# Low-part key products and cumulative-sum broadcasts over 128 rows instead of 64, in a two-layer hybrid decoder kernel

## The chip, the core and the metric

The kernel runs on one core of a Trainium2 chip. The core has a matrix engine (TensorE, PE in the rows, its weight loads PEld), VectorE (DVE), ScalarE (ACT), GpSimd (POOL), and a queue engine for transfers (SyncE, SP). The metric is the device time of one execution in microseconds, as the median of several runs.

## The reference, cut to what matters

Two layers run for a prompt of 512 tokens and a sample group of 8 x 4 = 32 tokens. The three branches of a layer share one normalised input `h`:

```python
A  = indexer-selected sparse GQA softmax attention (top-256 keys per query, 16 query heads, 4 key heads of 64)
B  = multi-scale causal pooling
C  = Mamba-2 SSD (32 heads of 64, state 128, chunks of 128, exact scan)
x += gate1 * (sum_b sigmoid(G_b) * (branch_b @ w_branch_b)) @ w_out
x += gate2 * ((silu(g) * a) @ ffn_down),   [a, g] = causal_dwconv3(h2 @ ffn_up)
```

Three places matter here. In the attention a score is `q . k` over 64 elements. In the indexer, which chooses the keys, a score is the sum over 8 heads of `w * relu(qi . ki)`, again over 64 elements. In the SSD branch the decay between two tokens of a chunk is `exp(cs[t] - cs[s])`, where `cs` is the cumulative sum of `dt * a` of one head over the tokens of its chunk.

## The kernel before

Tensors lie with channels on the 128 partitions and the 544 tokens along the row. Every large product is made in float32r with both operands split in a high and a low part: `gemm` (line 336 holds its matmul) makes `wh*xh`, `wh*xl` and `wl*xh` for each of 8 blocks of the contraction, in two halves of 272 columns. For each weight tile SP loads `raw`, ACT rounds it to `wh` (line 177) and DVE subtracts to get `wl` (line 322).

A layer runs `project`, `ssd`, `pool_branch`, `attention`, `merge_out`, `ffn`. Beside the products of a stage run side chains, written as generators in lanes; `pump` advances each lane by some steps before every product. While the SSD's input and gate weights are multiplied, the lanes make the indexer scores (`scores`) and the SSD heads (`ssd_chain`, `ssd_sample`). The top-k search of the indexer (lines 805 and 806, DVE) runs later, beside the branch products. A scheduler in the framework then sets the final order on each engine from its own model of durations; tiles come from rings of buffers, with a wait where a buffer is still in use.

The products that the change touches have a contraction of only 64:

- **Attention, line 1368** (`attn_scores`). A unit is one block of 128 queries (`i` = 0 to 3), one pair of key heads `p` and one pair of query rows `rp`: 16 units a layer. For each of its four query heads, `qs` holds the high part of the query in 64 partitions and the low part in the other 64. Line 1367 multiplies all 128 rows with `khh`, in which the high part of the keys stands twice. Line 1368 adds the high part of the query times the low part of the keys, `klo`, over the 64 partitions `es` of this head, into the same PSUM bank. `klo` holds two heads in one tile, one in each half. The number of columns is `nk` = 128 * (i + 1).
- **Indexer, line 783** (`scores`). The same construction: line 782 over 128 rows with `ikh`, line 783 over 64 rows with `ikl`, at 256, 384 and 512 columns, for 8 heads.
- **SSD, lines 977 and 1048**. `csT` holds the cumulative sums, one head to a row, high parts in rows 0 to 31 and low parts in rows 32 to 63. One column of `selc`, a matrix of zeros and ones, taken as a weight for all 128 output rows, broadcasts the row of one head to all partitions: 512 columns for the prompt (line 977, then subtracted from on DVE in line 981), 32 for the sample group (line 1048, eight in a row).

The softmax of a unit runs on DVE (mask and maximum, line 1373, which also frees the PSUM tile), ACT (line 1376) and DVE again; then PE transposes the result (line 1390) and multiplies with the values (line 1395). PSUM tiles `psg` come from a ring of two, shared by these scores and by `gemm`. Units 0 to 4 of a layer have one gate product each beside them (`filler`), and from unit 8 on the attention of the sample group runs beside them. The low keys are made by DVE in line 1260, four per layer.

Of the kernel before, what the change touches and what calls it, by code (L numbers as in the profile page):

```python
# [36 lines left out]
HC = T // 2  # L37
# [66 lines left out]
class Prog:  # L104
# [90 lines left out]
    def consts(self):  # L195
# [14 lines left out]
        nc.vector.memset(self.mean_w[:, 1:2], 1.0 / 512)  # L210
        self.selc = self.cp.tile([64, 32], F32R, name="selc")
        nc.vector.tensor_copy(self.selc, c[:64, C_SEL:C_SEL + 32])
        self.oh = self.cp.tile([32, 8, 64], BF16, name="oh")
# [21 lines left out]
    def ada(self, l, s, first=False):  # L235
        """modulation columns of two of the six chunks, in four groups of two channel tiles each."""
        nc, a = self.nc, self.a
# [102 lines left out]
    def gemm2(self, srcs, rhs, done=None):  # L340
        """two products, both for the first half of the tokens before the second half."""
        nc = self.nc
        self.pump()
        self.pump()
        K = len(rhs)
        ws, self.pre = self.pre or [self.weights(src, K * 128) for src in srcs], None
        os_ = [self.G() for _ in srcs]
        for c in range(2):
            for (wh, wl), o in zip(ws, os_):
                for k in range(K):  # L350
                    xh, xl = rhs[k]
                    for w, x, first, last in ((wh, xh, True, False), (wh, xl, False, False), (wl, xh, False, True)):
                        nc.tensor.matmul(o[:, c, :HC], w[:, k * 128:(k + 1) * 128], x[:, c * HC:(c + 1) * HC],  # L353
                                         start=(k == 0 and first), stop=(k == K - 1 and last))
            if done:
                done(os_, c)
        return os_
# [79 lines left out]
    def gemm_norm(self, l, srcs, rhs, gate, second):  # L437
        """the last two products of a sum into x, and the normalisation that follows."""
        st = {}

        def done(os_, c):
            for z, o in enumerate(os_):
                self.resid(l, 6 + z, o, gate, (c,))
            if second is not None:
                self.norm(l if second else l + 1, second, c, st)
        self.gemm2(srcs, rhs, done)
# [79 lines left out]

    # ---- attention projections, indexer scores
    def project(self):
# [17 lines left out]
        self.project_qi()  # L546
        # v, token-major
        wv = [self.weights(a["wv"][l, z], 1024) for z in range(2)]
# [70 lines left out]
    def dt_chain(self, kd):  # L619
# [73 lines left out]
        ct = self.csT = self.t("csT")  # L693
        cr = ct.bitcast(F32R)
        for so, do in ((o[:32, :], slice(0, 512)), (o2[:32, :32], slice(512, T))):
            self.copy("dt_chain20", cr[:32, do], so)
            self.E("dt_chain19").tensor_tensor(cr[32:64, do], so, ct[:32, do], op=OP.subtract)
        yield

    def scores(self):  # L700
# [3 lines left out]
        self.tp_ = []  # L704
        # sample group
        qs = self.t("qis")
# [55 lines left out]
        yield  # L762
        # prompt: both parts of a query head stacked against the high part of the keys
        khi, klo = self.t("ikh"), self.t("ikl")
# [6 lines left out]
        for hd in range(8):  # L771
# [6 lines left out]
            for i in PO:  # L778
# [3 lines left out]
                nc.tensor.matmul(ps[:, :nk], xr[:, ts], khr[:, :nk], start=True, stop=False)  # L782
                nc.tensor.matmul(ps[:, :nk], xr[o_, ts], klr[o_, :nk], start=False, stop=True)  # L783
                r = self.t("rel")
# [45 lines left out]

    # ---- SSD branch
    def conv(self, o, par, wb, nt, bb, st, so, i, width):
        """depthwise causal convolution of one channel tile; o: [128, 2, HC] in PSUM."""
        nc = self.nc
# [120 lines left out]
    def ssd_chain(self, q, jj, xs):  # L955
# [18 lines left out]
        for e in range(2):  # L974
            hd = 2 * j + e
            ps = self.P("ssd_chain2")
            nc.tensor.matmul(ps, self.selc[:, hd:hd + 1].to_broadcast([64, 128]), csr[:64, :512], start=True, stop=True)  # L977
            d = self.t("seg")
# [48 lines left out]
    def ssd_sample(self, q):  # L1027
# [19 lines left out]
        for i in range(8):  # L1047
            nc.tensor.matmul(ps[:, i * 32:(i + 1) * 32], self.selc[:, 8 * g + i:8 * g + i + 1].to_broadcast([64, 128]),
                             csr[:64, 512:], start=True, stop=True)
        ecs, mt = self.t("secs"), self.t("smt")  # L1050
# [88 lines left out]

    # ---- pooling branch  # L1140
    def pool_branch(self):
# [95 lines left out]

    # ---- attention
    def attention(self):
# [5 lines left out]
        for p in range(2):  # L1245
            nc.scalar.dma_start(kt[p], a["o_k"][l, p])
            nc.scalar.dma_start(vt[p][:, :512].rearrange("p (i c) -> p i c", i=2),
                                a["o_v"][l, p * 256:(p + 1) * 256].rearrange("(i p) c -> p i c", p=128))
        # high and low parts of the keys
        khh, klo = [], []  # L1250
        self.knew = self.s([128, 2, 32], "knew", bufs=1)
        for p in range(2):
            self.E("attention1").tensor_copy(self.knew[:, p, :], kt[p][:, 512:])
            lo = self.t("klo").bitcast(F32R)
            for e in range(2):
                hi = self.t("khh").bitcast(F32R)
                for z in range(2):
                    self.copy("attention9", hi[64 * z:64 * z + 64, :512], kt[p][64 * e:64 * e + 64, :512])
                s_ = slice(64 * e, 64 * e + 64)
                self.E("attention2").tensor_tensor(lo[s_, :512], kt[p][s_, :512], hi.bitcast(F32)[s_, :512], op=OP.subtract)  # L1260
                khh.append(hi)
            klo.append(lo)
        q = []
# [32 lines left out]
        self.E("attention6").tensor_scalar(nsq8, rq[:, 0:4], -0.125, None, op0=OP.mult)  # L1296
        # sample queries, normalised and laid out block-diagonally
        bc = [self.t("qbc0"), self.t("qbc1")]
# [44 lines left out]
    def attn_scores(self, u, q, khh, klo, sq8, nsq8):  # L1343
# [18 lines left out]
        for e in range(2):  # L1362
            ps = self.G()
            es = slice(64 * e, 64 * e + 64)
            for r2 in range(2):
                zs = slice((2 * e + r2) * 128, (2 * e + r2) * 128 + 128)
                nc.tensor.matmul(ps[:, r2, :nk], qr[:, zs], khh[2 * p + e][:, :nk], start=True, stop=False)  # L1367
                nc.tensor.matmul(ps[:, r2, :nk], qr[es, zs], klo[p][es, :nk], start=False, stop=True)  # L1368
            for r2 in range(2):
# [72 lines left out]
    def sample_scores(self, b, kv, P):  # L1442
        """rows of the scores: page half, key head pair, key head, token, query head."""
        nc = self.nc
# [79 lines left out]

    # ---- output projection of the merged branches
    def merge_out(self):
# [15 lines left out]

    # ---- feed-forward
    def ffn(self):
# [81 lines left out]
def _tiles(w):  # L1626
    """[K, M] -> [M/128, 128, K/128 * 128], tile rows in order of the contraction index within its block."""
    K, M = w.shape
# [7 lines left out]
def prep(x_prompt, x_sample, c_prompt, c_sample, cache_k, cache_v, cache_kidx, page_table,  # L1636
# [8 lines left out]
    out["cT"] = np.concatenate([c_prompt, c_sample], 0).T.reshape(8, 128, 9).transpose(1, 0, 2)  # L1645
    wa = w_ada.reshape(L, 4, 2, 128, 3, 2, 4, 256)  # l, k pair, k, row, set, chunk, group, column
    out["w_ada"] = wa.transpose(0, 4, 6, 1, 3, 2, 5, 7).reshape(L, 3, 16, 128, 1024)
# [119 lines left out]
```

## Time and profile before

| | |
|---|---|
| time, median of three runs | 3312.31 us (3304.55 to 3320.29) |
| span of the profiled execution | 3323.4 us |
| mean granted TensorE clock, share of full speed | 0.967 |
| PE / DVE / ACT / POOL busy | 97% / 67% / 38% / 27% |
| chain that ended last | PE 82%, DVE 4% |

The page gives the span of one execution. No separate time of that execution is listed; the span lies 11 us above the median and 3 us above the longest of the three runs. In the rows below, "64\*128" behind an instruction of PE means that its weights cover 64 rows and 128 columns of the array, "128\*128" all of it; this is called its form. PEclk is the granted clock: 1.00 is 2.4 GHz and 0.50 is 1.2 GHz.

### The profile page before, as it was taken

The page shows a single profiled execution, that of the slowest core. Times are in us where ns is not written, and L with a number is a line of the kernel's source. Part 1 is how long each engine was busy: PE and PEld are TensorE (multiplying, and loading weights), DVE is VectorE, ACT ScalarE, POOL GpSimd, SP SyncE. Part 2 cuts the span into 40 slices and gives each one's busy share as a digit, 9 for nine tenths or more (in the row PEclk, how much of TensorE's full clock was granted, in tenths as well). Part 3 has the DMA queues.
Part 4 walks back from the last instruction along what each step waited for, and adds up shares of the span by engine and source line. Part 5 has one row for each costly group of instructions (what it writes and reads, how often), then busy time and mean ns, then how long its engine had stood idle before and what let it go on. Part 6 is the DMA issues. An engine that isn't in the chain of part 4 may idle for free.

```text
span 3323.4 us, 62987 instructions
## 1 busy us (share of the span) xinstructions
PE 3240.0 (97%) x24322; PEld 2872.7 (86%) x24322; DVE 2229.5 (67%) x4817; ACT 1262.6 (38%) x2228; POOL 892.1 (27%) x1271
## 2 busy tenths in 40 slices
PE   7999999999999999999999999999999999999999
PEld 5987898999896598888989877888999956999999
DVE  4687778679876656444566777786799866564554
ACT  3344434333234534323343344433342345253432
POOL 1363435521021002111123544355120200031211
PEclk8998999999998899999999989999999989999999
DMA  6332323345532433545334323233343324333332
GB/s 218 108 100 75 103 76 102 115 130 186 167 109 91 157 124 113 149 141 151 115 107 118 89 80 101 84 99 113 97 126 115 92 90 161 116 74 87 86 96 76
DMA packets 303102, 376.85 MB, mean 113 GB/s; under 512 B 177362, under 2 KB 186930, under 8 KB 302802
## 3 DMA queue, kind: packets, MB, share of 16 engines
q1 hardware_dynamic: 116514, 315.94, 29.4%
q10 hardware_dynamic: 181216, 42.05, 6.2%
q0 software_dynamic: 5072, 14.83, 1.2%
q8 instruction: 192, 3.15, 0.4%
q14 instruction: 108, 0.88, 0.1%
HBM read 330.34 MB, written 33.79 MB: 110 GB/s over the span
## 4 chain that ended last, share of the span: by engine, by line
PE 82%; DVE 4%; issue 1%; ACT 1%; POOL 1%; DMA 1%; ACTq 0%; SPq 0%; POOLq 0%; DVEq 0%
PE psg L336 61%; PE psb L253 2%; PE psg L353 2%; PE psb L1395 1%; PE psg L1368 1%; PE psa L1390 1%; PE psg L1367 1%; PE psb L1005 1%; PE psa L1087 1%; PE psg L1455 1%; PE psb L991 1%; PE psb L1014 1%; DVE wl L322 1%; PE psa L977 1%; PE psa L783 1%
## 5 line engine op out<-in xcount | busy, mean ns | idle before, releaser
L177 ACT ACTIVATE wh<-raw 128x1024 fp32r<-128x1024 f32 (+2 forms) x434 | 424.8, 980 | 1208.7 <-PE psg L336 930.7
L336 PE MATMUL psg<-hh,wh 128*128 128x272 f32 x4064 | 868.5, 294 | 4.2 <-ACT cacc L838 3.3
L336 PE MATMUL psg<-hl,wh 128*128 128x272 f32 x4064 | 858.9, 291 | 0.0
L336 PE MATMUL psg<-hh,wl 128*128 128x272 f32 x4064 | 857.3, 291 | 0.0
L322 DVE TENSOR_TENSOR wl<-raw,wh 128x1024 fp32r<-128x1024 f32 (+2 forms) x434 | 510.8, 1177 | 356.4 <-ACT wh L177 346.8
L336 PEld LDWEIGHTS psg<-hh,wh 128*128 128x128 f32 x4064 | 643.9, 190 | 60.9 <-issue 31.8
L336 PEld LDWEIGHTS psg<-hl,wh 128*128 128x128 f32 x4064 | 645.7, 190 | 19.0 <-issue 17.4
L336 PEld LDWEIGHTS psg<-hh,wl 128*128 128x128 f32 x4064 | 644.2, 190 | 20.6 <-issue 19.0
L840 POOL COPY sti<-cu 128x32 f32<-128x32 f32 x136 | 91.8, 675 | 594.7 <-ACT cu L177 594.5
L845 DVE SCALAR_TENSOR_TENSOR cacc<-cu,half,cacc 128x511 f32<-128x511 f32 x144 | 136.5, 948 | 8.0 <-ACT cacc L838 7.6
L336 PE MATMUL psg<-fh,wh 128*128 128x272 f32 x648 | 135.5, 291 | 2.6 <-DVE resid L460 2.6
L454 DVE SCALAR_TENSOR_TENSOR x<-psg,mod,x 128x272 f32<-128x272 f32 x64 | 32.0, 499 | 156.0 <-PE psg L336 146.9
L854 ACT ACTIVATE th<-cacc 128x544 f32<-128x544 f32 x92 | 60.5, 657 | 198.7 <-DVE cacc L848 190.2
L336 PE MATMUL psg<-fl,wh 128*128 128x272 f32 x648 | 134.1, 288 | 0.0
L336 PE MATMUL psg<-fh,wl 128*128 128x272 f32 x648 | 133.7, 288 | 0.0
L336 PEld LDWEIGHTS psg<-fh,wh 128*128 128x128 f32 x648 | 101.1, 188 | 14.3 <-issue 7.5
L336 PE MATMUL psg<-oh,wh 128*128 128x272 f32 x512 | 113.2, 299 | 0.0
L336 PE MATMUL psg<-ol,wh 128*128 128x272 f32 x512 | 110.7, 294 | 0.0
L336 PE MATMUL psg<-oh,wl 128*128 128x272 f32 x512 | 109.4, 293 | 0.0
L855 DVE SCALAR_TENSOR_TENSOR cacc<-th,cacc 128x544 f32<-128x544 f32 x92 | 72.7, 790 | 49.4 <-ACT th L854 49.1
L985 POOL TENSOR_TENSOR seg<-seg,cb 128x512 f32<-128x512 f32 x64 | 88.9, 1392 | 61.9 <-ACT seg L984 55.4
L336 PEld LDWEIGHTS psg<-fl,wh 128*128 128x128 f32 x648 | 101.9, 188 | 0.0
(468 smaller groups left out, 6313.7 us busy)
## 6 DMA issues: line engine op xcount, KB each, us to landing
raw<-wk SPq DMA_DIRECT2D x326, 512.0 KB, 3.6
raw<-w_ada SPq DMA_DIRECT2D x96, 512.0 KB, 3.6
h<-h SPq DMA_DIRECT2D x64, 256.0 KB, 3.9
raw<-wk SPq DMA_DIRECT2D x64, 256.0 KB, 2.8
o_ssds<-hn ACTq DMA_DIRECT2D x64, 256.0 KB, 2.2
raw<-wd SPq DMA_DIRECT2D x32, 448.0 KB, 3.5
kvr<-ckv SPq DMA_DIRECT2D x48, 256.0 KB, 3.9
kvw<-ckv SPq DMA_DIRECT2D x48, 256.0 KB, 3.7
```

The source lines that it names most:

```text
L177: self.nc.scalar.activation(out, src, AF.Copy)
L253: nc.tensor.matmul(ps[g:g + 32, :], self.sc[:, k, :], raw[:, q * 512:(q + 1) * 512], start=(k < 4), stop=(k >= 4))
L322: self.last_wl = self.E("weights1").tensor_tensor(wl[:, :n], raw[:, :n], wh[:, :n].bitcast(F32), op=OP.subtract).ins
L336: nc.tensor.matmul(o[:, c, :HC], w[:, k * 128:(k + 1) * 128], x[:, c * HC:(c + 1) * HC], start=(k == 0 and first), stop=(k == K - 1 and last))
L353: nc.tensor.matmul(o[:, c, :HC], w[:, k * 128:(k + 1) * 128], x[:, c * HC:(c + 1) * HC], start=(k == 0 and first), stop=(k == K - 1 and last))
L783: nc.tensor.matmul(ps[:, :nk], xr[o_, ts], klr[o_, :nk], start=False, stop=True)
L840: self.E("conv1").tensor_copy(st[:, i, :, W - 1:], new)
L845: self.E("conv3").scalar_tensor_tensor(acc[:, s:512], u[:, :512 - s], wc, acc[:, s:512], op0=OP.mult, op1=OP.add)
L854: nc.scalar.activation(th, acc, AF.Tanh)
L855: self.E("silu21").scalar_tensor_tensor(acc, th, 1.0, acc, op0=OP.add, op1=OP.mult)
L977: nc.tensor.matmul(ps, self.selc[:, hd:hd + 1].to_broadcast([64, 128]), csr[:64, :512], start=True, stop=True)
L985: self.E("ssd_chain5").tensor_tensor(d[:, :512], d[:, :512], cb[:, :512], op=OP.mult)
```

## The change

All four products go over 128 rows. `csT` gets zeros in rows 64 to 127 and `selc` 128 rows (its source has zeros there). In the indexer only the slices go away: `ki` already stands in both halves of the partitions, so `ikl` is whole. In the attention each key head gets a `klo` of its own with its low part in both halves, so that four tiles are made by eight subtractions instead of two by four, always on DVE. The product then also holds the low part of the query times the low part of the keys. The rest of the diff removes comments and is left out here.

```diff
-        self.selc = self.cp.tile([64, 32], F32R, name="selc")
-        nc.vector.tensor_copy(self.selc, c[:64, C_SEL:C_SEL + 32])
+        self.selc = self.cp.tile([128, 32], F32R, name="selc")
+        nc.vector.tensor_copy(self.selc, c[:, C_SEL:C_SEL + 32])
...
         cr = ct.bitcast(F32R)
+        nc.vector.memset(ct[64:128, :], 0.0)
...
-                nc.tensor.matmul(ps[:, :nk], xr[o_, ts], klr[o_, :nk], start=False, stop=True)
+                nc.tensor.matmul(ps[:, :nk], xr[:, ts], klr[:, :nk], start=False, stop=True)
...
-            nc.tensor.matmul(ps, self.selc[:, hd:hd + 1].to_broadcast([64, 128]), csr[:64, :512], start=True, stop=True)
+            nc.tensor.matmul(ps, self.selc[:, hd:hd + 1].to_broadcast([128, 128]), csr[:, :512], start=True, stop=True)
...
-            nc.tensor.matmul(ps[:, i * 32:(i + 1) * 32], self.selc[:, 8 * g + i:8 * g + i + 1].to_broadcast([64, 128]),
-                             csr[:64, 512:], start=True, stop=True)
+            nc.tensor.matmul(ps[:, i * 32:(i + 1) * 32], self.selc[:, 8 * g + i:8 * g + i + 1].to_broadcast([128, 128]),
+                             csr[:, 512:], start=True, stop=True)
...
-            lo = self.t("klo").bitcast(F32R)
             for e in range(2):
                 hi = self.t("khh").bitcast(F32R)
+                lo = self.t("klo").bitcast(F32R)
+                s_ = slice(64 * e, 64 * e + 64)
                 for z in range(2):
-                    self.copy("attention9", hi[64 * z:64 * z + 64, :512], kt[p][64 * e:64 * e + 64, :512])
-                s_ = slice(64 * e, 64 * e + 64)
-                self.E("attention2").tensor_tensor(lo[s_, :512], kt[p][s_, :512], hi.bitcast(F32)[s_, :512], op=OP.subtract)
+                    self.copy("attention9", hi[64 * z:64 * z + 64, :512], kt[p][s_, :512])
+                for z in range(2):
+                    nc.vector.tensor_tensor(lo[64 * z:64 * z + 64, :512], kt[p][s_, :512],
+                                            hi.bitcast(F32)[s_, :512], op=OP.subtract)
                 khh.append(hi)
-            klo.append(lo)
+                klo.append(lo)
...
-                nc.tensor.matmul(ps[:, r2, :nk], qr[es, zs], klo[p][es, :nk], start=False, stop=True)
+                nc.tensor.matmul(ps[:, r2, :nk], qr[:, zs], klo[2 * p + e][:, :nk], start=False, stop=True)
```

In the changed program the scheduler keeps the order of SP word for word, and that of PE but for small shifts. Behind line 697 its line numbers are higher by one to three.

DVE, layer 1, second pair of key heads, beside the last steps of the top-k search: each subtraction into `klo` (`kr1` are the keys, `khh` their high part) stands alone, two into one tile. Before:

```order
L1260 TENSOR_TENSOR klo_10307<-kr1_10288,khh_10308 64x512
L806 MATCH_REPLACE wks_1804<-mxs_10129,wks_1804 32x1028
L262 TENSOR_TENSOR mod_107<-psb_10211,par_105 128x2x18
L1260 TENSOR_TENSOR klo_10307<-kr1_10288,khh_10312 64x512
L805 MAX mxs_10132<-wks_1804 32x8
```

The same place in the changed program:

```order
L1262 TENSOR_TENSOR klo_10312<-kr1_10289,khh_10311 64x512 x2
L807 MATCH_REPLACE wks_1805<-mxs_10130,wks_1805 32x1028
L262 TENSOR_TENSOR mod_107<-psb_10212,par_105 128x2x18
L1262 TENSOR_TENSOR klo_10318<-kr1_10289,khh_10317 64x512 x2
L1233 SCALAR_TENSOR_TENSOR gt_10195<-gt_10195,psg_10224 128x544
```

Each subtraction has become two, each pair has a tile of its own, and what stands around them is as before.

PE, layer 2, the second unit of the attention (`qbc` are the norms of the sample queries, `hh`, `hl`, `wh` a gate product). Before:

```order
L1367 MATMUL psg<-khh,qs 128x128
L1368 MATMUL psg<-klo,qs 128x128
L1367 MATMUL psg<-khh,qs 128x128
L1368 MATMUL psg<-klo,qs 128x128
L1307 MATMUL psb<-cst,qbc_30705 128x32 x4
L1307 MATMUL psb<-cst,qbc_30706 128x32 x4
L1367 MATMUL psg<-khh,qs 128x128
L1368 MATMUL psg<-klo,qs 128x128
```

The same place in the changed program, from the last pair of scores on:

```order
L1369 MATMUL psg<-khh,qs 128x128
L1370 MATMUL psg<-klo,qs 128x128
L336 MATMUL psg<-hh,wh 128x272 x2
L336 MATMUL psg<-hl,wh 128x272 x2
L336 MATMUL psg<-hh,wl 128x272 x2
L336 MATMUL psg<-hh,wh 128x272 x2
L336 MATMUL psg<-hl,wh 128x272 x2
L336 MATMUL psg<-hh,wl 128x272 x2
L336 MATMUL psg<-hh,wh 128x272 x2
L1310 MATMUL psb<-cst,qbc_30719 128x32 x4
```

The eight small products have moved behind the scores, into the gate product; the alternation of the two score products is unchanged.

## Rows read from the trace of the kernel before

**Rows 1.** The page: busy time of the engines, and the chain that ended last.
```profile
PE 3240.0 (97%) x24322; PEld 2872.7 (86%) x24322; DVE 2229.5 (67%) x4817; ACT 1262.6 (38%) x2228; POOL 892.1 (27%) x1271
...
PE 82%; DVE 4%; issue 1%; ACT 1%; POOL 1%; DMA 1%; ACTq 0%; SPq 0%; POOLq 0%; DVEq 0%
```
**Rows 2.** PE timeline, SSD: start us, busy us, line, tiles, form, count.
```profile
459.02 0.41 PE L336 MATMUL psg<-oh,wl 128*128 128x272 f32 x2
459.27 0.41 PE L336 MATMUL psg<-oh,wh 128*128 128x272 f32 x2
459.61 0.49 PE L977 MATMUL psa<-csT,selc 64*128 64x512 f32 x1
460.04 0.52 PE L336 MATMUL psg<-ol,wh 128*128 128x272 f32 x2
460.39 0.41 PE L336 MATMUL psg<-oh,wl 128*128 128x272 f32 x2
```
**Rows 3.** PE timeline, SSD: a product of 512 columns over 96 rows.
```profile
515.84 0.40 PE L1099 MATMUL psb<-sxst,bbd 96*128 96x512 f32 x1
516.08 0.29 PE L336 MATMUL psg<-hl,wh 128*128 128x272 f32 x1
516.21 0.41 PE L336 MATMUL psg<-hh,wl 128*128 128x272 f32 x2
```
**Rows 4.** PE timeline, token-major values: 256 columns, all into one bank.
```profile
109.55 0.28 PE L559 MATMUL psa<-wh,hl 128*128 128x256 f32 x1
109.67 0.28 PE L559 MATMUL psa<-wl,hh 128*128 128x256 f32 x1
```
**Rows 5.** PE timeline, attention, 512 columns; then the weight load of one of them.
```profile
1102.10 0.50 PE L1367 MATMUL psg<-khh,qs 128*128 128x512 f32 x1
1102.54 0.50 PE L1368 MATMUL psg<-klo,qs 64*128 64x512 f32 x1
1102.96 0.50 PE L1367 MATMUL psg<-khh,qs 128*128 128x512 f32 x1
...
1102.53 0.18 PEld L1368 LDWEIGHTS psg<-klo,qs 64*128 64x128 f32 x1 [0.25 <-issue]
```
**Rows 6.** All products of line 1368 in the trace: count, durations min/median/max in ns, forms.
```profile
L1368 PE MATMUL psg<-klo,qs x128: 322/439/792, 971.2 to 2785.6; 64*128 64x128 f32 x32, 64*128 64x256 f32 x32, 64*128 64x384 f32 x32, 64*128 64x512 f32 x32
```
**Rows 7.** PE timeline, attention: 128 and 256 columns in both forms, in two stretches.
```profile
982.88 0.33 PE L1367 MATMUL psg<-khh,qs 128*128 128x128 f32 x1
983.14 0.32 PE L1368 MATMUL psg<-klo,qs 64*128 64x128 f32 x1
...
1021.38 0.38 PE L1368 MATMUL psg<-klo,qs 64*128 64x256 f32 x1
1021.70 1.09 PE L1390 MATMUL psa<-cst,S 128*128 128x128 f32 x8
1022.55 0.36 PE L1367 MATMUL psg<-khh,qs 128*128 128x256 f32 x1
```
**Rows 8.** PE timeline, attention, at a granted clock of 0.50.
```profile
1035.68 0.56 PE L1367 MATMUL psg<-khh,qs 128*128 128x256 f32 x1
1036.17 0.58 PE L1368 MATMUL psg<-klo,qs 64*128 64x256 f32 x1
```
**Rows 9.** Stretches: busy us (count) of PE, PEld, DVE, ACT, POOL; PEclk, DMA share, GB/s.
```profile
150.00:700.00 550.00, 541.37 (x3940) 470.06 (x3939) 413.56 (x799) 210.43 (x358) 250.42 (x285) 0.98 0.31 96
...
1026.00:1057.00 31.00, 30.21 (x148) 15.53 (x147) 19.05 (x88) 12.18 (x37) 2.12 (x8) 0.50 0.01 1
1057.00:1111.00 54.00, 52.57 (x494) 28.93 (x492) 40.72 (x188) 34.20 (x97) 6.17 (x24) 1.00 0.42 140
...
750.00:960.00 210.00, 210.00 (x1579) 187.98 (x1578) 183.83 (x288) 61.61 (x89) 32.10 (x37) 1.00 0.53 169
```
**Rows 10.** What PE waited for in the attention of layer 1: total us, times, longest.
```profile
PE psg L1367 <- DVE qs L1360: 1.6, 2, 0.8
```
**Rows 11.** The low keys on DVE (ns min/median/max).
```profile
L1260 DVE TENSOR_TENSOR klo<-kr,khh x8: 675/687/691, 792.5 to 2543.3; 64x512 fp32r<-64x512 f32 x8
```

More of the change, by code (lines that the diff above doesn't have):

```diff
@@ L1363, in attn_scores @@
             ps = self.G()
-            es = slice(64 * e, 64 * e + 64)
             for r2 in range(2):
```

## The prediction

> **What bounds the kernel now.** The first view is the page's busy shares and the chain that ended last: PE is busy 97% of the span and holds 82% of the chain, and no other engine holds over 4% of it [rows 1]. So I read PE, and since a busy PE may be standing still between two products, I read it by start times in the timeline, not by durations. The plain pace is set by `gemm`: two products of 272 columns over 128 rows start 0.25 us after the two before (459.02 to 459.27), 0.125 us each [rows 2]. Around line 977, a 64-row product of 512 columns, three steps are longer: the pair ahead takes 0.34 us (459.27 to 459.61), the product 0.43, the pair behind 0.35 [rows 2]. The comparison is another float32r product of 512 columns between `gemm` products, line 1099. It covers 96 rows, its next neighbour starts 0.24 us later (515.84 to 516.08), and that neighbour keeps 0.13 [rows 3]. So a form of 96 rows between forms of 128 costs nothing extra, and a form of 64 rows costs (0.34 - 0.25) + (0.43 - 0.24) + (0.35 - 0.25) = 0.38 us, that is 0.19 us for each of its two sides.
>
> Two readings of that cost have to be told apart. One is that the second product of a sum waits for the first in its PSUM bank. Line 977 adds to nothing, and line 559, which adds 24 products into one bank in a row, starts one every 0.12 us at 256 columns [rows 4]. So it is the change of form: PE ends what is under way, then loads weights with nothing beside it. The weight load of line 1368 shows this from the other side; it begins 0.25 us after the load engine was free, waiting for nothing that the profile names [rows 5].
>
> **What the change removes.** I price it by sides, places where a 64-row product stands next to one of another form. There are 128 products of line 1368 [rows 6], 64 of line 977 (32 heads, two layers) and 48 of line 783 (8 heads, three query blocks, two layers), each with two sides, and the 64 of line 1048 stand in runs with 20 outer sides: 500. In 4 of them two products of line 977 face each other, and in 48 the neighbour has a narrower form (line 1395's 128\*64, line 1455's 128\*32 and the like), so that a change of form stays. 448 go away, and the order of the changed program has the same neighbours but for a handful. 222 of them lie in the indexer and the SSD, 226 in the attention.
>
> The price of a side: 0.19 us from rows 2 and 3. In the attention at 512 columns each product takes 0.42 to 0.44 us [rows 5] against 0.24 [rows 3]: 0.19 again, since between two changes each product carries one. At 128 columns a product takes 0.26 us and eight of one form take 0.85, 0.11 each: 0.15 a side [rows 7]. At a granted clock of 0.50, 1.2 GHz, a product of 256 columns takes 0.49 us [rows 8]; in one form it would take about twice the 0.12 of [rows 4], an estimate: 0.25 a side.
>
> - Indexer and SSD: 222 x 0.19 = 42 us.
> - Attention: 62 sides at 128 columns x 0.15 = 9.3; 40 sides in the two stretches at half clock (1026 to 1057 us and its twin in layer 2) x 0.25 = 10; the other 124 x 0.19 = 23.6. Together 43 us.
>
> That is 85 us of PE's time. A higher form costs nothing that I find: line 1099 with 96 rows is at 0.24 us where the column count at 0.125 us for 272 gives 0.235 [rows 2, 3].
>
> **How much of it reaches the end.** In the stage with indexer and SSD, PE is busy 541 of 550 us and DVE 414 [rows 9]. Taking 21 us out of 550 leaves DVE at 78%, and the weights come from engines that were ahead. I take 95%: 40 us for both layers. In the attention the softmax follows each score product. Between 1057 and 1111 us DVE is busy 41 of 54 us; 36 sides x 0.19 = 7 us less for PE leaves 47, DVE at 87%. Between 1026 and 1057 us it is 19 of 31, or of 26 after 20 x 0.25 [rows 9]. No engine is full, but the two PSUM tiles of the scores come free only through DVE's maximum, and PE already waits there for `qs` for up to 0.8 us at a time [rows 10]. So I take three quarters: 32 us.
>
> **What it adds.** Eight more subtractions of 64x512 at 0.687 us each make 5.5 us on DVE [rows 11]. They stand beside the branch and gate products, where PE is busy 210 of 210 us and DVE 184 [rows 9]; 2.75 us more per layer fit into the 26 us that DVE has left there, and `klo`, first written at 792.5 us [rows 11], is first read at 971.2 [rows 6]. Without that cover they cost 5.5 us. The two memsets of 64x544 lie between 0 and 0.7 us each, the price of such a subtraction, which reads two operands besides [rows 11]; they stand in the chain of `dt`, under `gemm`. I take zero for both. Two more tiles of the ring of 49 are held through the attention; the transfers for the sample group then wait for other buffers, and since the order of SP is the same I take no cost, up to a few us.
>
> A rule of the Trainium skill speaks against the change. First the row: line 1368 starts 0.44 us after line 1367 and its weights begin to load only 0.01 us before [rows 5], so the two do not overlap. The page "TensorE: Matmul & The Clock Gate", Part 3 (packing small matmuls), says that products in different row groups of the array run at the same time and that a weight load overlaps running products only if the row group differs. By it the 64-row products could be hidden beside their neighbours, and widening them would cost time (the last rival); this trace shows no such overlap at these lines.
>
> **The sum.** 40 + 32 + 0 = 72 us. Against the profiled span that is 3323.4 - 72 = 3251 us. The span is 11 us above the median of the runs, and a difference carries over, so I set it against the median: 3312.3 - 72 = **3240 us**.
>
> **The rivals.**
>
> *The softmax takes over the attention.* PE's gain there turns into waits for DVE and ACT, in particular in units 5 to 7 of each layer, which have no gate product or sample work beside them. For it: the two PSUM tiles, the waits for `qs` [rows 10]. Against it: DVE is at 61 to 75% [rows 9] and ACT lower. Then 0 to 15 us of the attention remain: 3312 - 40 - 8 = 3264 us, from 3257 to 3272. Chance 0.13.
>
> *The clock stays up.* From 1026 to 1057 us the granted clock is 0.50 [rows 9], after units that alternate between forms with no `gemm` between them. If the denser products keep it at 1.00, the 26 us left there become 26 x 0.32 / 0.49 = 17 [rows 7, 8], but DVE's 19 hold it: 7 us for each of the two layers. With all of the 85: 3312 - 85 - 14 = 3213 us. Chance 0.06.
>
> *The change does nothing on PE.* The drain would come from something else that these products share, such as a weight taken from a tile that was just written. Against it: the pair behind line 977 pays too, and it shares nothing with it [rows 2]. Then 0 to 6 us are added on DVE: 3315 us. Chance 0.04.
>
> *Slower: the clock stays down.* PE ends its scores earlier, stands waiting for the softmax more often, and the clock of 1.2 GHz, now granted in 31 us of a layer's attention, holds for all of its 190 us. A product of 256 columns takes 0.49 us at it against 0.32 [rows 7, 8], so each us loses about 0.35. It decides from about 255 us of additional time at that clock, where 0.35 x 255 = 89 eats the 72 us and 17 more; all that is left of both attention stages, some 300 us, would give 3312 - 72 + 0.35 x 300 = 3345 us. Against it: with as many changes of form, 1057 to 1111 us has 1.00 [rows 9]. Chance 0.02.
>
> *Slower: the 64 rows were hidden.* If they ran beside their neighbours, as the rule above has it, 128 products of line 1368 and 48 of line 783 would come on top at 0.11, 0.12, about 0.17 and 0.24 us [rows 3, 4, 7]: 20.5 + 8.5 = 29, 3341 us. Rows 5 speak against it. Chance 0.01.
>
> **How the numbers follow.** The forecast itself, 85 us of PE's time of which 60 to 100% arrive, has 0.74 and reaches from 3227 to 3261. The range takes in the first two rivals: down to 3213 less half of the runs' spread of 16 us, 3205; up to 80% of the indexer and SSD alone, 34 us, 3278, rounded to 3280. What a measurement can tell from no change is about 0.5%, 17 us. All of the forecast and the first two rivals is faster by more: 0.93. No change 0.04, slower 0.03.
>
> **What would show it.** In the changed trace lines 784, 978 and 1370 have the form 128\*128; a 512-column product between `gemm` products takes 0.23 to 0.24 us to the next start and the pairs around it 0.25; scores of 512 columns follow each other at 0.24 while PE does not wait. PEld loses its "issue" time at these lines. The stage from 150 to 700 us shortens by 20 us and each attention by 15 to 20; everything else keeps its length. I am wrong if the starts keep 0.43 us at 128 rows, if the attention keeps its length with new waits for line 1373's maximum, or if the granted clock there falls below 0.9 on the mean.

## The result, and the profile after

The changed kernel takes 3217.0 us (3214.0 to 3219.4, four runs), the kernel before on the same chip 3311.2 us (four runs). The ratio is 0.970, with a 95% interval from 0.968 to 0.973: 94 us less between the medians, where 72 were forecast (3240 us). The profiled execution of the changed kernel spans 3217.6 us at a mean granted clock of 0.985.

The page, busy time of the engines, as in [rows 1]:

```profile
PE 3117.6 (97%) x24322; PEld 2834.3 (88%) x24322; DVE 2229.4 (69%) x4827; ACT 1258.1 (39%) x2228; POOL 892.9 (28%) x1271
```

PE has the same 24322 instructions and is as full as before, and DVE, ACT and POOL do what they did: PE got shorter, by 122 us of busy time, and its weight loads by 38. (The chain that ended last is of no use here; the page follows it over only 42% of the span.)

PE timeline in the SSD, a product of 512 columns between `gemm` products, as in [rows 2] (start us, busy us, line, tiles, form, count):

```profile
453.50 0.42 PE L336 MATMUL psg<-hh,wl 128*128 128x272 f32 x2
453.75 0.29 PE L336 MATMUL psg<-hh,wh 128*128 128x272 f32 x1
453.88 0.40 PE L978 MATMUL psa<-csT,selc 128*128 128x512 f32 x1
454.11 0.29 PE L336 MATMUL psg<-hh,wh 128*128 128x272 f32 x1
454.24 0.41 PE L336 MATMUL psg<-hl,wh 128*128 128x272 f32 x2
454.49 0.41 PE L336 MATMUL psg<-hh,wl 128*128 128x272 f32 x2
```

The step into the product is 0.13 us, out of it 0.23, and the next pair keeps its 0.25. All three extra amounts of [rows 2] are gone.

PE timeline in the attention at 512 columns, as in [rows 5], and the weight load of the first product of line 1370:

```profile
1045.89 0.39 PE L1370 MATMUL psg<-klo,qs 128*128 128x512 f32 x1
1046.12 0.40 PE L1369 MATMUL psg<-khh,qs 128*128 128x512 f32 x1
1046.36 0.40 PE L1370 MATMUL psg<-klo,qs 128*128 128x512 f32 x1
1046.60 0.33 PE L1523 MATMUL psb<-cst,so 128*128 128x64 f32 x2
...
1045.66 0.19 PEld L1370 LDWEIGHTS psg<-klo,qs 128*128 128x128 f32 x1
```

The scores follow each other at 0.23 to 0.24 us instead of 0.42 to 0.44, and the weights are loaded 0.23 us ahead of their product, where [rows 5] has 0.01.

All products of line 1370, as in [rows 6], with who waited for them (us, times). Behind it stand two lines of the same view of line 1368 before: the idle time of the weight loads ahead of it, and the same waiter:

```profile
L1370 PE MATMUL psg<-klo,qs x128: 272/310/401, 941.3 to 2680.5; 128*128 128x128 f32 x32, 128*128 128x256 f32 x32, 128*128 128x384 f32 x32, 128*128 128x512 f32 x32
...
DVE S L1375: 34.2, 25
```
```profile
issue: 18.7, 78
...
DVE S L1373: 78.2, 53
```

The weight loads stood idle for 18.7 us at 78 places, waiting for nothing named; the view of line 1370 lists no idle time at all. DVE's maximum now waits 34 us for the scores in all (25 times), where it waited 78 us (53 times): the softmax came closer to PE, but did not take over.

Stretches with the same work in the two traces (us, then busy us and count of PE, PEld, DVE, ACT, POOL, then PEclk, DMA share, GB/s). First the changed kernel: the stage that answers to 150 to 700 us in [rows 9], the two attentions, then in layer 1 the attention's units 6 to 8, 9 to 13 and 14:

```profile
142.80:671.20 528.40, 516.05 (x3946) 466.55 (x3946) 413.70 (x801) 209.95 (x359) 251.60 (x285) 0.99 0.31 100
...
941.20:1095.10 153.90, 143.94 (x1364) 101.26 (x1363) 112.70 (x515) 94.56 (x260) 19.03 (x71) 0.99 0.38 126
2540.10:2699.50 159.40, 144.84 (x1362) 101.95 (x1360) 120.95 (x534) 94.12 (x259) 19.25 (x68) 0.98 0.37 124
...
988.90:1010.50 21.60, 18.97 (x163) 10.84 (x163) 20.19 (x97) 14.38 (x47) 2.35 (x8) 1.00 0.06 22
1010.50:1057.40 46.90, 43.97 (x477) 26.45 (x477) 38.54 (x177) 32.45 (x92) 5.96 (x24) 1.00 0.46 153
1057.40:1070.70 13.30, 12.85 (x143) 7.55 (x141) 9.40 (x40) 7.54 (x20) 1.19 (x5) 1.00 0.76 259
```

Then the kernel before: its two attentions, and in layer 1 the same units:

```profile
971.00:1154.90 183.90, 178.48 (x1362) 114.20 (x1360) 113.93 (x518) 96.58 (x260) 18.90 (x72) 0.86 0.32 105
2619.20:2804.50 185.30, 177.33 (x1362) 115.21 (x1360) 119.18 (x530) 95.30 (x259) 19.13 (x67) 0.87 0.33 107
...
1025.20:1058.90 33.70, 32.72 (x163) 17.10 (x163) 20.97 (x97) 14.66 (x46) 2.12 (x8) 0.54 0.00 1
1058.90:1109.50 50.60, 49.34 (x479) 27.17 (x477) 38.54 (x175) 32.45 (x91) 6.17 (x24) 1.00 0.42 139
1109.50:1129.00 19.50, 19.50 (x142) 10.45 (x140) 9.80 (x40) 8.05 (x21) 1.18 (x5) 0.65 0.52 179
```

The first stage lost 22 us (550 to 528), layer 1's attention 30 and layer 2's 26. Inside the attention the loss is uneven. Units 9 to 13, at full clock in both, lost 3.7 us; units 6 to 8, at 0.54 before and 1.00 now, lost 12; unit 14, at 0.65 before, lost 6. So a part of the gain looks like clock. PE is no longer full in units 6 to 8: 19.0 of 21.6 us, with DVE at 20.2.

Where the time went, by the start of the same `gemm` product in both traces, is 106 us between the two spans: 6 before the first such product (the profile of before is late there by itself: the kernel before with moved gate products, below, has the same code in that stretch and starts it 7 us earlier), 22 and 18 in the stages with indexer and SSD, 30 and 26 in the attentions, next to nothing in the branch products, the merge and the ffn, and some 4 in small pieces. The medians differ by 94; the profile of before was 11 us longer than its median.

What stayed: the waits for `qs` of [rows 10], and the subtractions of [rows 11], now sixteen. The first row is total us, times and longest wait, the second ns min/median/max:

```profile
PE psg L1369 <- DVE qs L1363: 1.6, 2, 0.8
```
```profile
L1262 DVE TENSOR_TENSOR klo<-kr,khh x16: 678/686/691, 764.1 to 2465.9; 64x512 fp32r<-64x512 f32 x16
```

### The profile page after: what moved, and what is told of

The parts are those of the page before. It is cut to its first block, busy times and chain, and to the rows that moved or that the text cites. A ratio compares the mean times of both kernels' runs of the same rounds, so it can differ in the third digit from the quotient of the medians.

```text
span 3217.6 us, 63012 instructions
## 1 busy us (share of the span) xinstructions
PE 3117.6 (97%) x24322; PEld 2834.3 (88%) x24322; DVE 2229.4 (69%) x4827; ACT 1258.1 (39%) x2228; POOL 892.9 (28%) x1271
## 5 line engine op out<-in xcount | busy, mean ns | idle before, releaser
L336 PEld LDWEIGHTS psg<-hl,wh 128*128 128x128 f32 x4064 | 644.1, 189 | 15.9 <-issue 14.4
```

## The experiments

The theory: a product of 64 rows between products of 128 costs 0.19 us on each side, and the attention's gain is these sides and, in part, clock. The rivals: the softmax holds the attention; the 64-row products had been running beside their neighbours; the gain is clock alone, or the full height of 128 rows is what counts. Each ratio is to the kernel before, run beside it.

**The three parts, each alone.** The attention part alone (`klo` whole, line 1368 over 128 rows):

> The kernel before with the attention's part of the change alone (line 1368 over 128 rows, four klo tiles made by eight subtractions a layer). Theory (a cost for each side at which the form changes, plus the clock): 226 sides go, 43 us, and the two stretches of 31 us at a granted clock of 0.50 rise, 7 us each: 57 us less than before, 3254 us (3245 to 3264). Rival, the softmax holds the attention: about 32 us less, 3279 us; then most of what the whole change gained beyond the forecast would have to come from the indexer and the SSD.

Measured: 3259.2 us, ratio 0.986 (0.984 to 0.987). The indexer part alone (line 783):

> The kernel before with the indexer's part alone (line 783 over 128 rows, no other instruction added). Theory: 94 sides x 0.19 us = 18 us less, 3293 us. If the second product of a sum were slow because it waits for the first in its PSUM bank, the time would stay at 3311 us.

Measured: 3295.5 us, ratio 0.996 (0.994 to 0.998). The SSD part alone (`selc`, `csT`, lines 977 and 1048):

> The kernel before with the SSD's part alone (lines 977 and 1048 over 128 rows, zeros below the sums). Theory: 128 sides x 0.19 us = 24 us less, 3287 us. Line 977 adds to nothing, so the rival of the PSUM bank gives 3311 us. The three parts should add up to the whole change, 94 us.

Measured: 3285.4 us, ratio 0.994 (0.992 to 0.996). The medians are 52, 16 and 26 us below that of before, 94 together, as the whole change. By the ratios it is 47, 13 and 21, together 81, against 99 for the whole, with 6 to 8 us of uncertainty on each; the 18 us that are left over are somewhat more than these uncertainties make together, about 13. So the parts add up or nearly so, indexer and SSD meet their forecast, and the attention exceeds its 32 us.

**Half the sides, 64 rows kept.** The two high products first, then the two low ones, so that low products stand next to each other:

```diff
                 nc.tensor.matmul(ps[:, r2, :nk], qr[:, zs], khh[2 * p + e][:, :nk], start=True, stop=False)
+            for r2 in range(2):
+                zs = slice((2 * e + r2) * 128, (2 * e + r2) * 128 + 128)
                 nc.tensor.matmul(ps[:, r2, :nk], qr[es, zs], klo[p][es, :nk], start=False, stop=True)
```

> The kernel before with 64 rows everywhere, but for each pair of query heads the two products with the high keys come first and then the two with the low keys, so that two 64-row products stand next to each other. The work is the same; 128 of the attention's 228 sides go. Theory (the cost lies in the change of form, not in the product): half of what the attention's part gives, 24 us for the sides and up to 14 more if the clock rises: 3273 to 3287 us. Rival (a 64-row product is slow by itself, whatever stands beside it): 3311 us.

Measured: 3280.4 us, ratio 0.992 (0.989 to 0.995). PE timeline and, behind it, units 6 to 8 of layer 1 and of layer 2:

```profile
1010.87 0.48 PE L1367 MATMUL psg<-khh,qs 128*128 128x256 f32 x2
1011.28 0.50 PE L1370 MATMUL psg<-klo,qs 64*128 64x256 f32 x2
1011.71 0.65 PE L1397 MATMUL psb<-PT,vr 128*64 128x256 f32 x4
...
1013.20:1034.50 21.30, 19.54 (x162) 11.13 (x162) 19.92 (x97) 14.48 (x47) 2.28 (x8) 1.00 0.01 2
2643.00:2668.70 25.70, 24.45 (x163) 14.00 (x163) 20.52 (x97) 14.40 (x46) 2.35 (x8) 0.73 0.01 2
```

Not the 64 rows cost time but the change: two low products together take 0.43 us, where each alone took about 0.32. And units 6 to 8 of layer 1, with 64-row products and half of their sides left, take 21.3 us at a clock of 1.00, as in the changed kernel (21.6). In layer 2 the clock there is 0.73. With all the sides in place the same follows as an estimate: the ten stretches of units 6 to 8 in the five kernels with the attention of before lie on a line from 27.2 us with 13.7 at half clock to 33.6 with 30.7, which leads to about 22 with none. So of the 12 us that these units gained some 11 are clock; once it is up, the sides there cost next to nothing, since DVE is busy 20 of 21 us.

**96 rows in the SSD.** The SSD part with 96 rows in place of 128:

```diff
-            nc.tensor.matmul(ps, self.selc[:, hd:hd + 1].to_broadcast([64, 128]), csr[:64, :512], start=True, stop=True)
+            nc.tensor.matmul(ps, self.selc[:, hd:hd + 1].to_broadcast([96, 128]), csr[:96, :512], start=True, stop=True)
```

> The SSD's part alone, but over 96 rows instead of 128. Theory (what costs is a change between forms, and 96 rows count as the same form as 128, as line 1099 does): the same as the part over 128 rows, 3285 us, and the pairs of gemm around line 977 keep 0.25 us. Rival (only the full array is free of it): near the 3311 us of before.

Measured: 3291.3 us (3283.7 to 3305.2), ratio 0.993 (0.990 to 0.996). The PE timeline, and behind it the attention of layer 2, whose code is that of before:

```profile
430.24 0.29 PE L336 MATMUL psg<-ol,wh 128*128 128x272 f32 x1
430.37 0.40 PE L978 MATMUL psa<-csT,selc 96*128 96x512 f32 x1
430.60 0.29 PE L336 MATMUL psg<-ol,wh 128*128 128x272 f32 x1
430.73 0.41 PE L336 MATMUL psg<-oh,wl 128*128 128x272 f32 x2
...
2580.50:2784.80 204.30, 196.90 (x1363) 124.09 (x1361) 119.77 (x536) 96.27 (x260) 19.84 (x70) 0.77 0.30 99
```

A product of 96 rows starts 0.13 us after its neighbour and gives way after 0.23, as one of 128 rows. So it is the 64-row form, not the unused part of the array. The profiled execution was the longest of the four, and shows why: the untouched attention of layer 2 ran at 0.77 and took 204 us, where it took 185 at 0.87 before. That is clock without any change of code.

**Low products of two heads side by side (indexer).** Two heads are made together, their high products first, then the two 64-row products, which lie in different halves of the array and go to different PSUM banks:

```diff
+                pss = [self.P("scores6"), self.P("scores4")]
+                for ps, (xr, o_) in zip(pss, xrs):
+                    last = nc.tensor.matmul(ps[:, :nk], xr[:, ts], khr[:, :nk], start=True, stop=False).ins
+                for ps, (xr, o_) in zip(pss, xrs):
+                    with self.tc.issue_after(last):
+                        last = nc.tensor.matmul(ps[:, :nk], xr[o_, ts], klr[o_, :nk], start=False, stop=True).ins
```

> The kernel before with the indexer's heads taken two at a time: both products with the high keys, then directly behind each other the two 64-row products with the low keys, one over rows 0 to 63 and one over rows 64 to 127, into different PSUM banks. If 64-row products in different halves of the array run at the same time, the second starts with the first, and the pair of 512 columns takes one product's time. If they run one after the other, it starts 0.21 to 0.24 us later. In time: 48 of 94 sides go, 9 us, 3302 us; with overlap 24 pairs save another 0.18 us each, 4 us, 3298 us. The start times in the trace decide, not the total.

Measured: 3298.0 us, ratio 0.995 (0.993 to 0.997). PE timeline of one such group:

```profile
327.95 0.47 PE L785 MATMUL psb<-ikh,qs 128*128 128x512 f32 x1
328.27 0.40 PE L785 MATMUL psa<-ikh,qs 128*128 128x512 f32 x1
328.59 0.49 PE L788 MATMUL psa<-ikl,qs 64*128 64x512 f32 x1
328.60 0.50 PE L788 MATMUL psb<-ikl,qs 64*128 64x512 f32 x1
329.02 0.39 PE L785 MATMUL psa<-ikh,qs 128*128 128x256 f32 x1
```

All 24 pairs start 3 to 4 ns apart: two 64-row products in different halves do run at the same time. The rival of hidden products is right for this order, and wrong for the order of before, where the neighbours cover all rows. The gain is that of the indexer part alone within the intervals. The four products take 0.32 + 0.32 + 0.43 = 1.07 us, against 4 x 0.235 = 0.94 over 128 rows, so widening remains the better form.

**The attention split in two.** The wide low product only in the units of the second query block (units 4 to 7), and only in the other twelve:

```diff
-                nc.tensor.matmul(ps[:, r2, :nk], qr[es, zs], klo[p][es, :nk], start=False, stop=True)
+                ks = slice(0, 128) if i == 1 else es
+                nc.tensor.matmul(ps[:, r2, :nk], qr[ks, zs], klo[2 * p + e][ks, :nk], start=False, stop=True)
```

> The attention's part alone, the wide low product only in the units of the second query block (256 columns), which make up the first half of the stretches at half clock; the klo tiles are made as in the change. About 56 sides go, a third of them in those stretches: 12 us. If the alternation of forms in these units is what lets the clock fall, up to 14 us more: 3285 to 3299 us, and the low clock of some 30 us is gone from both attentions.

Measured: 3291.2 us, ratio 0.993 (0.991 to 0.995). The other way about (`i != 1`):

> The complement: the wide low product in all units but those of the second query block. About 170 sides go, 31 us. If the clock falls because of the units of the second block, the stretch at 0.50 stays: 3280 us. If it falls because of what the attention as a whole asks of PE, it goes here too: 3268 us.

Measured: 3268.8 us, ratio 0.987 (0.985 to 0.988). Units 6 to 8 of layer 1 in the one and in the other, then in layer 2 of the kernel with side-by-side products in the indexer, whose attention is that of before:

```profile
1012.10:1039.20 27.10, 24.83 (x162) 13.26 (x163) 20.32 (x97) 14.33 (x47) 2.30 (x8) 0.75 0.05 17
```
```profile
1015.20:1042.10 26.90, 25.89 (x162) 15.23 (x163) 20.73 (x97) 14.52 (x46) 2.20 (x8) 0.68 0.01 2
```
```profile
2660.10:2687.30 27.20, 26.05 (x161) 14.04 (x162) 20.45 (x97) 14.40 (x46) 2.25 (x8) 0.75 0.00 1
```

Both expectations on the clock were met in part only: with either half these units stand at 0.68 to 0.79 in the two layers, where the first expectation had the low clock gone and the second had it stay at 0.50 or go. How much of that is due to the halves cannot be told, because kernels with the attention of before show 0.54 to 0.75 there. What the two runs do show is that neither half brings these units to the 0.92 to 1.00 that they have with the whole attention part. By the ratios the halves gain 23 and 44 us, together 67, against 47 for the attention part whole: what each gives in part overlaps.

**Dense products beside the bare units.** In both kernels the three gate products that stand ahead of the first unit stand beside units 5 to 7 (`NF`). `AS` is the unit behind which the top-k search of the sample group is finished and its attention may begin; it moves from 4 to 7 with them, and DVE ends that search in layer 1 some 76 us into the attention in place of 24, so the runs move two things. The kernel before first:

```diff
-AS, AR = 4, 6
+AS, AR = 7, 6
...
-NF = 3
+NF = 0
```

> The kernel before, its 64-row products kept; only the gate products of the attention move: three that stood ahead of the first unit stand beside units 5 to 7, so that units 0 to 7 have one each. Theory A, the low clock belongs to score units that alternate between forms with nothing dense between them: the stretch of 0.50 at 1026 to 1057 us and its twin go, each was worth 7 to 14 us, so 3311 - 14 to 28 = 3283 to 3297, unless the norms ahead of the first unit now lie open. Theory B, the low clock goes with the 64-row form itself and not with what stands beside the units: the stretch stays, 3311 within 6 us.

Measured: 3306.7 us, ratio 0.999 (0.997 to 1.000). Its windows over units 5 to 8 of layer 1, then over units 0 to 4:

```profile
1000.10:1045.10 45.00, 43.57 (x337) 32.72 (x335) 33.45 (x124) 21.99 (x59) 3.36 (x12) 1.00 0.33 107
...
942.80:1000.10 57.30, 56.01 (x328) 48.97 (x329) 33.30 (x160) 21.31 (x61) 8.99 (x27) 0.84 0.15 48
```

That is no change that can be told. The expectation of 3283 to 3297 missed, though its first half came true: the low clock in units 5 to 8 is gone, with all 64-row products kept. It came back in units 0 to 4, at 0.84, and PE now waits once for the softmax's first queries, which the three gate products had covered, 2.4 us where its longest such wait was 0.8 [rows 10]:

```profile
PE psg L1367 <- DVE qs L1360: 2.4, 1, 2.4
```

The changed kernel with the same move:

> The changed kernel with the same move of three gate products. The changed kernel has 3.4 us at half clock per attention, so by both theories there is at most 3 us of clock to gain: 3217 within 6 us. Slower than 3223 would mean that the three gate products ahead of the first unit cover the norms of the queries, and that price would then have to be added back in the run of the kernel before with the same move.

Measured: 3231.3 us, ratio 0.976 (0.973 to 0.978), 14 us above the changed kernel, which has hardly any low clock to win back (3.4 us in layer 1 and 6.8 in layer 2). The move brought low clock with it, 12 and 15 us at half clock, mostly in units 0 to 4: at 0.35 us each that is some 6 of the 14, an estimate. In the kernel before it took away more than it brought, 98 us at half clock in both layers becoming 54, some 15 us, and its other costs ate most of that. It is no better version.

**The subtractions twice.** In the changed kernel:

```diff
-                for z in range(2):
+                for z in (0, 1, 0, 1):
                     nc.vector.tensor_tensor(lo[64 * z:64 * z + 64, :512], kt[p][s_, :512],
```

> The changed kernel with each of its 16 subtractions into the low keys made twice: 16 x 0.34 to 0.69 us = 5.5 to 11 us more on DVE, beside the gate products, twice the addition of the change. Theory, they are hidden: 3217, the ratio to the kernel before 0.970 to 0.972. Rival, DVE is late in that stage: 3222 to 3228.

Measured: 3220.0 us, ratio 0.972 (0.970 to 0.974). Their row, and the stage of layer 1 in which they are made, here and in the changed kernel:

```profile
L1262 DVE TENSOR_TENSOR klo<-kr,khh x32: 666/686/691, 770.1 to 2481.3; 64x512 fp32r<-64x512 f32 x32
...
726.00:936.00 210.00, 210.00 (x1578) 188.01 (x1577) 189.00 (x295) 61.95 (x89) 32.15 (x37) 1.00 0.51 170
```
```profile
720.00:930.00 210.00, 210.00 (x1588) 188.98 (x1587) 186.17 (x291) 62.94 (x90) 30.66 (x38) 1.00 0.51 171
```

The 3 us between the medians lie inside the spread, and by the medians alone the case is open. The trace decides it: PE is full in that stage in both, and the same `gemm` products start at a constant distance in the two traces while the subtractions run, 5.88 to 5.89 us from 755 to 895 us of the changed kernel and 9.8 to 9.9 us from 2280 to 2539. Sixteen additional subtractions are hidden. So are the eight of the change: from the kernel before to the changed one the distance stays at 28.6 us over 720 to 900 us of the kernel before.

## Why the prediction was right, and where it was not

**The price of a side** was right. The three steps around line 978 lost 0.09, 0.19 and 0.10 us, which is the 0.38 that was read from [rows 2, 3], and regrouping shows that it is the change of form that costs. The place is no exception: in either trace 36 such products have `gemm` products on both sides at full clock, and the medians of their three steps are 0.34, 0.43 and 0.36 us before and 0.25, 0.23 and 0.25 after. At 128 columns the step from one score product to the next fell from 0.25 to 0.11 us, 0.14 a side, where 0.15 was forecast.

**Indexer and SSD** were right: 40 us forecast, 42 by the medians of the two parts alone, 40 by the trace. Some 4 or 5 us of the 40 are probably clock. The kernel before with the moved gate products has the code of before in this stage of layer 1, and its profile is 3.6 us shorter there (546.4 us in place of 550), with 10 us at half clock in place of 24. The changed kernel has the same 10 us and takes 527.5: the sides alone gave 19 of that layer's 22 us. The row of the former:

```profile
140.20:686.60 546.40, 536.02 (x3940) 468.57 (x3939) 413.35 (x799) 210.18 (x358) 249.84 (x285) 0.99 0.30 97
```

**The attention** was mis-sized: 32 us forecast, 52 by the median of that part alone, 56 by the trace (30 and 26 us, where each layer was to lose 15 to 20). The step that failed is "I take three quarters", with the clock set aside as a rival of 0.06: both parts of it were off, in opposite directions. Five kernels have the attention of before (before, the indexer part alone, the SSD part alone, 96 rows, side by side). Their profiles give the length of a stage against the time in it at half clock (in a row of stretches that time is nearly 2 x (1 - PEclk) x length):

| | layer 1: length, at half clock (us) | layer 2 |
|---|---|---|
| before | 183.9, 50.4 | 185.3, 47.7 |
| SSD part alone | 176.4, 27.3 | 188.7, 56.5 |
| indexer part alone | 177.3, 34.1 | 176.7, 27.3 |
| SSD with 96 rows | 178.4, 37.6 | 204.3, 95.7 |
| indexer side by side | 176.4, 28.6 | 184.2, 44.4 |
| changed kernel | 153.9, 3.4 | 159.4, 6.8 |
| attention part alone | 156.8, 16.4 | 158.0, 8.9 |
| subtractions twice | 155.1, 8.5 | 160.0, 13.7 |
| regrouped | 157.3, 3.4 | 167.5, 23.8 |
| units 4 to 7 alone | 170.7, 18.9 | 178.1, 32.3 |
| the other twelve units | 161.3, 20.5 | 162.5, 15.9 |

A straight line through the first five has each of them within 1 us, rises by 0.33 us for each us at half clock in layer 1 and by 0.40 in layer 2, close to the 0.35 that the prediction used for its slower rival, and gives 167 and 166 us with none. The changed kernel, brought to no half clock in the same way, is at 153 and 157. So the sides gave 14 + 9 = 23 us (the two other kernels with this attention come to 27 and 26), little over half of the 43 and not three quarters: the softmax does hold part of it, as feared, in units 6 to 8 above all. In the same way regrouping, with half of the sides gone, gives 19 us, units 4 to 7 alone 3, the other twelve units 22: where DVE is nearly full, a side that goes brings little. The clock gave the rest, some 30 us: 3 to 16 us at half clock in the six stages of the three kernels with the changed attention, 27 to 96 in the ten of the five with that of before. It is an accounting by regression on single profiles; the split is good to some us.

**The clock rival** is what came true. The measured 3217 us lies below the 3227 to 3261 that were given to the forecast itself, and 4 us above this rival's 3213, which had a chance of 0.06. That the number is so near is luck: the rival has 85 us of sides and 14 of clock, and the profiles give some 60 (36 in the indexer and the SSD, 23 to 27 in the attention) and some 35. So is its price for units 6 to 8: 5 us of sides and 7 of clock were put down per layer, 12 were measured, though some 11 of them are clock. What it left out are unit 14 (6 and 3 us) and the first ones of layer 2. Its evidence was weighed wrongly. I had held against a change of clock that 1057 to 1111 us has as many changes of form at 1.00 [rows 9], but that stretch has the sample group's work between the scores. The bare units 5 to 7 have neither that nor a gate product. That this is the difference is argued, not shown: with gate products beside them and the search of the sample group moved, their low clock went, but other units got it.

**What the clock follows** is shown only in part. With all score products over 128 rows it is 0.95 to 0.99 on the mean in each of the six stages in question. Regrouping put it at 1.00 in units 6 to 8 of layer 1 with 64-row products in place, and so did the moved gate products in both layers, so it is not the height of the products as such. Beyond that the profiles are too few: the kernels with the same attention differ from one another in its clock (27 to 96 us at half clock per layer), the attentions with units 4 to 7 widened (19 and 32) and with moved gate products (36 and 19) lie partly inside that, and why it varies is open; no run here took that apart.

**The additions on DVE** at nothing: right, by the doubled subtractions. The memsets and the two more tiles of the ring were not tried alone.

**The other rivals.** That the softmax takes over was half right in size, since 16 to 20 of the 43 us of sides did not come back, and wrong as an outcome: DVE's maximum still waits for the score products, 34 us in place of 78, and PE's waits for `qs` are unchanged. That the change does nothing on PE, and that the 64 rows had been hidden, fell with the first trace. By the prediction's own wording the rule on which the latter leans is about products in different row groups of the array, and the neighbours of these products, lines 782 and 1367, cover all rows: it did not speak against the change. "The clock stays down" fell too: 10 us at half clock in both attentions, in place of 98.

## What to carry to other kernels

Price a product of another form by the starts of its two neighbours, not by its duration: here each place where the form changes cost 0.14 to 0.19 us at full clock, and by that price 448 of them were 85 us of PE time that no wait of PE named; only the weight loads' idle time without a releaser hinted at it. In the dense stage nearly the whole price came back, some 36 of 42 us; where a softmax follows each product, somewhat over half of it did. Where the granted clock of a stage is below 1.00 and the change makes PE stand still less, the clock belongs into the sum as a term with a range, here some 0.3 to 0.4 us for each us at half clock, and not among the remote rivals. And before a run is said to move the clock, look how far it moves in profiles whose code for that stage is the same.

## What the runs showed of the hardware

Two 64-row products in different halves of the array, adjacent and into different PSUM banks, start 3 to 4 ns apart and share their time, in float32r too. The Trainium skill, page "TensorE: Matmul & The Clock Gate", Part 3, gives about 4 ns between the starts of products in different row groups, and the trace agrees. Between products over all rows a 64-row product overlapped nothing in the trace of before, and both of its sides were paid for: 0.34, 0.43 and 0.36 us where 0.25, 0.23 and 0.25 are taken after the change.

A product over 96 rows of 512 columns had no such price, though a quarter of the array is empty in it: 0.13 us in and 0.23 us out, as with 128 rows.

The attention's clock can fall much further than the first profile showed: 96 of 204 us at half clock in layer 2 with its code unchanged, in the longest of that kernel's four executions.
